# Differential attention scores on all 128 rows of the array, from keys and queries split into high and low parts

## The chip, the cores and the metric

One core of one Trainium2 chip. The metric is the device time of one launch in microseconds (us); lower is better.

## What is computed

One decoder layer on 256 tokens of width 2048, all in float32. Three parts follow each other with residual adds: a mixer with two attention branches, cross-attention into 256 memory tokens, and a gated MLP with a short causal convolution. The change lies in the first branch, differential attention: 8 heads, each with two softmax maps of dimension 64 and values of 128.

```python
z = h @ w_in                       # h: normalised x
qa, ka, va, qb, kb, vb, ga, gb = split_columns(z, IN_WIDTHS)
qa = partial_rope(qa.reshape(b, s, 8, 2, 64), cos, sin)   # first 16 of 64
ka = partial_rope(ka.reshape(b, s, 8, 2, 64), cos, sin)
...
sc = einsum('bhmqd,bhmkd->bhmqk', q, k) * 64 ** -0.5
p = softmax(where(causal, sc, -inf))
a = p[:, :, 0] - lam * p[:, :, 1]
o = einsum('bhqk,bhkv->bhqv', a, v)
```

## The kernel before

**The products.** Every weight product goes through `product` (L208): a unit of 512 output columns, accumulated in two PSUM banks (one per 128 tokens) over 16 blocks of 128 rows. The weights come in pieces of 1 MB on SP's queue. `split_w` (L191) makes two float32r parts of each half piece: ACT casts the high part (L193), DVE subtracts for the low part (L194), and `mm3` (L197) issues three matmuls of 512 columns, high by high, high by low and low by high (L199 to L201). A unit of the mixer has 96 of them; they are called plain matmuls below. The high and low tiles have three buffers each, and PSUM has four banks for products and four (`sm_tile`) for everything small.

**The order.** The program emits a unit, and after every half piece `tick` (L92) advances queued generators (`spawn`, L89) such as one stage of an attention head. The units of the mixer come as qa0, ka0, va0, qa1, ka1, va1, qb0, kb0, vb0, qb1, kb1, vb1 and eight gates. This emitted order is then reordered per engine by a scheduler with a time model of its own (all engines but SP); what stands in a row on an engine is fixed when the program is built, and each engine takes its instructions in that row. A unit reuses the PSUM banks of the unit two before it, so qb0 needs the banks of ka1.

**Queries and keys of branch A.** `proj_T` (L274) scales the two banks on ACT into two SBUF tiles (L280), `rope` (L252) rotates them with four GpSimd operations each, PE transposes four 128x128 blocks per tile (L289), and DVE copies them out (L291). Queries and keys then have features on partitions, head by head, 64 rows per map.

**A head.** `diff_head` (L332) has four stages. Scores: per map two float32 matmuls on 64 rows (L340), of 128 and 256 key columns, then DVE adds the mask (L343) and takes maxima (L346), ACT exponentiates (L352), DVE normalises and subtracts the maps (L354 to L360). Then PE transposes the weights (L322 to L324) and DVE copies them (L326). Then six matmuls with the values (L369 to L371), sums of squares on ACT (L174) and a norm on DVE and ACT (L376 to L388). Last, two transposes (L393) and a split (L398, L399). Two chains of two heads each run after va0 and again after va1.

**Stick-breaking queries and keys.** `proj_F` (L297) does without PE: ACT scales the bank in place, DVE transposes 32x32 blocks (`turn`, L127), and 16 transfers on the GpSimd queue (`regroup`, L131) put the blocks in their places.

Of the kernel before, what the change touches and what calls it, by code (L numbers as in the profile page):

```python
# [9 lines left out]
F32 = mybir.dt.float32  # L10
F32R = mybir.dt.float32r
AF = mybir.ActivationFunctionType
ALU = mybir.AluOpType
# [3 lines left out]
P = 128  # L17
S = 256
NT = S // P
# [4 lines left out]
U = 512  # L24
# [4 lines left out]
ROT = 16  # L29
HALF = ROT // 2  # L30
# [15 lines left out]
def hybrid_layer(ctx: ExitStack, tc: tile.TileContext, x, xT, mem, memT, gmix, par, gfin,  # L46
                 w_in, w_pa, w_pb, w_out, w_xq, w_xkv, w_xo, w_up, w_dn, out):
    nc = tc.nc
# [3 lines left out]
    b4 = ctx.enter_context(tc.tile_pool(name="b4", bufs=34))  # L52
    wk = ctx.enter_context(tc.tile_pool(name="wk", bufs=7))
    st = ctx.enter_context(tc.tile_pool(name="st", bufs=4))
# [14 lines left out]
    ident = cst.tile([P, P], F32, name="ident")  # L69
# [19 lines left out]
    def spawn(gen, delay=0):  # L89
        tasks.append([clock[0] + delay, gen])  # L90
# [16 lines left out]
    def chunk_tile(name, shape):  # L107
        return b4.tile(shape, F32, tag="b4", name=name)

    def sm_tile(name):  # L110
        return ps_sm.tile([P, U], F32, tag="sm", name=name)
# [15 lines left out]
    def turn(blk, src, t):  # L127

        nc.vector.transpose(out=blk[:, :, t * P:(t + 1) * P], in_=src.rearrange("p (f c) -> p f c", c=P))  # L129

    def regroup(dst, blk):  # L131


        q = P // 4
        d, s = (v.rearrange("p f (t c) -> p (f t) c", t=NT) for v in (dst, blk))
        for a in range(4):
            for b in range(4):
                nc.gpsimd.dma_start(out=d[b * q:(b + 1) * q, :, a * q:(a + 1) * q],  # L138
                                  in_=s[a * q:(a + 1) * q, :, b * q:(b + 1) * q])

    def flip_tile(name):
        return chunk_tile(f"{name}_blk", [P, U // P, S])
# [109 lines left out]
    def rope(z, t):  # L252
        v = z.rearrange("p (m d) -> p m d", d=64)
        a = wk.tile([P, 8, ROT], F32, tag="rope", name="rope_a", bufs=2)
        b = wk.tile([P, 8, ROT], F32, tag="rope", name="rope_b", bufs=2)
        c = col("rc", t * ROT, ROT).unsqueeze(1).broadcast_to([P, 8, ROT])
        s = col("rs", t * ROT, ROT).unsqueeze(1).broadcast_to([P, 8, ROT])
        nc.gpsimd.tensor_tensor(out=a, in0=v[:, :, 0:ROT], in1=c, op=ALU.mult)
        nc.gpsimd.tensor_tensor(out=b[:, :, 0:HALF], in0=v[:, :, HALF:ROT], in1=s[:, :, 0:HALF],
                                op=ALU.mult)  # L260
        nc.gpsimd.tensor_tensor(out=b[:, :, HALF:ROT], in0=v[:, :, 0:HALF], in1=s[:, :, HALF:ROT],
                                op=ALU.mult)
        nc.gpsimd.tensor_tensor(out=v[:, :, 0:ROT], in0=a, in1=b, op=ALU.add)

    def proj_T2(ps, r, name):

        dst = [None, None]
        z = chunk_tile(f"{name}_z", [P, NT, U])
        for t in range(NT):
            nc.scalar.activation(out=z[:, t], in_=ps[t], func=AF.Copy, scale=r[:, t:t + 1])  # L270
        spawn(transposed(dst, z, 0, name), 2)
        return dst

    def proj_T(ps, r, name, rotate=False):  # L274

        dst = chunk_tile(name, [P, 4, S])
        zs = []
        for t in range(NT):
            z = wk.tile([P, U], F32, tag="w2", name=f"{name}_z")
            nc.scalar.activation(out=z, in_=ps[t], func=AF.Copy, scale=r[:, t:t + 1])  # L280
            if rotate:
                rope(z, t)
            zs.append(z)

        def rest():
            for t in range(NT):
                pt = sm_tile(f"{name}_tp")
                for h in range(4):
                    nc.tensor.transpose(out=pt[:, h * P:(h + 1) * P],  # L289
                                        in_=zs[t][:, h * P:(h + 1) * P], identity=ident)  # L290
                nc.vector.tensor_copy(out=dst[:, :, t * P:(t + 1) * P],  # L291
                                      in_=pt.rearrange("p (h s) -> p h s", h=4))
            yield 0
        spawn(rest(), 2)
        return dst

    def proj_F(ps, r, name, box, i):  # L297


        blk = flip_tile(name)  # L300
        for t in range(NT):
            nc.scalar.activation(out=ps[t], in_=ps[t], func=AF.Copy, scale=r[:, t:t + 1])
            turn(blk, ps[t], t)

        def rest():
            box[i] = chunk_tile(name, [P, 4, S])
            regroup(box[i], blk)
            yield 0
        spawn(rest(), 1)

# [21 lines left out]
    def diff_head(h):  # L332
        qT, kT, v, hh = qa[h // 4], ka[h // 4], va[h // 4], h % 4

        at = (slice(0, P), slice(P, 3 * P))
        sc = [sm_tile(f"sa{m}") for m in range(2)]
        nm = st.tile([P, 2, NT], F32, tag="nm", name="nm")
        for m in range(2):
            for i in range(NT):
                nc.tensor.matmul(sc[m][:, at[i]], lhsT=qT[m * 64:(m + 1) * 64, hh, i * P:(i + 1) * P],  # L340
                                 rhs=kT[m * 64:(m + 1) * 64, hh, 0:(i + 1) * P], start=True, stop=True)
            dg = sc[m].rearrange("p (i k) -> p i k", i=2)[:, :, 0:P]
            nc.vector.tensor_tensor(out=dg, in0=dg, in1=mask_le.unsqueeze(1).broadcast_to([P, 2, P]),  # L343
                                    op=ALU.add)
            for i in range(NT):
                nc.vector.tensor_reduce(out=nm[:, m, i:i + 1], in_=sc[m][:, at[i]], op=ALU.max,  # L346
                                        axis=AX, negate=True)
        p = [wk.tile([P, 3 * P], F32, tag="w2", name=f"pa{m}") for m in range(2)]
# [42 lines left out]
        pt = sm_tile("oaT")  # L391
# [3 lines left out]
        if oaT[h // 2] is None:  # L395
            oaT[h // 2] = act_tile(f"oaT{h // 2}")
        dst = oaT[h // 2]
        nc.scalar.activation(out=dst[:, 0, j], in_=pt[:, 0:S], func=AF.Copy, scale=gsub)  # L398
        nc.vector.scalar_tensor_tensor(out=dst[:, 1, j], in0=pt[:, 0:S], scalar=gsub,  # L399
                                       in1=dst[:, 0, j].bitcast(F32), op0=ALU.mult,  # L400
# [57 lines left out]
    def unit(u, name, **kw):  # L458
        return product(hT, w_in, u, KD, name, **kw)

    def chain(stage, items):
        for i in items:
            yield from stage(i)
            yield 1
# [7 lines left out]
    pq = unit(0, "qa0", pieces=[1, 1] + [2] * 7, before=first, heap=True)  # L472
# [15 lines left out]
    pk = unit(2, "ka0", before=lambda k0: input_sumsq(x, r0ss, k0 // KB, "r0"))  # L488
    r0 = rstd(r0ss, NT, D, "r0")
    r0a = scaled(r0, 64 ** -0.5, "r0a")  # L490
    r0b = scaled(r0, 128 ** -0.5, "r0b")
    qa, ka, va, qb, kb, vb = ([None, None] for _ in range(6))
    for i in range(2):
        qa[i] = proj_T(unit(i, f"qa{i}") if i else pq, r0a, f"qaT{i}", True)
        ka[i] = proj_T(unit(2 + i, f"ka{i}") if i else pk, r0, f"kaT{i}", True)
        va[i] = proj_n(unit(4 + i, f"va{i}"), r0, f"va{i}")
        spawn(chain(diff_head, (4 * i, 4 * i + 2)))
        spawn(chain(diff_head, (4 * i + 1, 4 * i + 3)), 2)
    for i in range(2):
        proj_F(unit(6 + i, f"qb{i}"), r0b, f"qbT{i}", qb, i)  # L500
        proj_F(unit(8 + i, f"kb{i}"), r0, f"kbT{i}", kb, i)
# [85 lines left out]
    for g in range(2):  # L587
        po = sm_tile("ox").rearrange("p (m s) -> p m s", m=2)
        for m in range(2):
            h = 2 * g + m  # L590
# [171 lines left out]
```

## Time and profile before

| | |
|---|---|
| median of 3 runs | 1493.68 us (1493.48 to 1493.75) |
| profiled execution | 1493.29 us, its span 1491.5 us |
| PE busy | 1475.6 us (99%) |
| DVE, ACT, POOL busy | 929.6, 788.9, 342.7 us |
| HBM traffic | 192 GB/s over the span |

PE's ends are modelled and its matmuls overlap, so its work is read from the spacing of their starts, not from durations. The mixer's first six units, with the heads among them, take the span's first 160 us.

### The profile page before, as it was taken

The page shows a single profiled execution, that of the slowest core. Times are in us where ns is not written, and L with a number is a line of the kernel's source. Part 1 is how long each engine was busy: PE and PEld are TensorE (multiplying, and loading weights), DVE is VectorE, ACT ScalarE, POOL GpSimd, SP SyncE. Part 2 cuts the span into 40 slices and gives each one's busy share as a digit, 9 for nine tenths or more (in the row PEclk, how much of TensorE's full clock was granted, in tenths as well). Part 3 has the DMA queues.
Part 4 walks back from the last instruction along what each step waited for, and adds up shares of the span by engine and source line. Part 5 has one row for each costly group of instructions (what it writes and reads, how often), then busy time and mean ns, then how long its engine had stood idle before and what let it go on. Part 6 is the DMA issues. An engine that isn't in the chain of part 4 may idle for free.

```text
span 1491.5 us, 17974 instructions
## 1 busy us (share of the span) xinstructions
PE 1475.6 (99%) x6648; PEld 1217.4 (82%) x6648; DVE 929.6 (62%) x1219; ACT 788.9 (53%) x1094; POOL 342.7 (23%) x576
## 2 busy tenths in 40 slices
PE   8999999999999999999999999999999999999997
PEld 6878788888888888888888888888888888888886
DVE  5566675655444566775576767767776776645552
ACT  6455555456554444664565555555655555444441
POOL 0202040400000240341004344434434443000010
PEclk9999999999999999999999999999999999999999
DMA  9544455554555566975456666666667666655561
GB/s 350 190 148 170 167 177 193 190 187 163 194 197 192 197 223 227 303 234 204 141 175 215 218 225 224 197 227 217 217 219 225 224 194 228 219 194 198 201 234 73
DMA packets 60391, 304.61 MB, mean 204 GB/s; under 512 B 13200, under 2 KB 13200, under 8 KB 27536
## 3 DMA queue, kind: packets, MB, share of 16 engines
q1 hardware_dynamic: 43488, 286.13, 55.5%
q0 software_dynamic: 16384, 16.81, 4.4%
q8 instruction: 52, 0.85, 0.2%
q10 hardware_dynamic: 432, 0.53, 0.1%
q14 instruction: 35, 0.29, 0.1%
HBM read 284.54 MB, written 2.10 MB: 192 GB/s over the span
## 4 chain that ended last, share of the span: by engine, by line
PE 97%; ACT 1%; issue 1%; DVE 0%; DMA 0%; POOLq 0%; POOL 0%; DVEq 0%; SPq 0%
PE up_mm L201 11%; PE up_mm L200 11%; PE up_mm L199 11%; PE dn_mm L199 5%; PE dn_mm L200 5%; PE dn_mm L201 5%; PE g_mm L200 4%; PE g_mm L201 4%; PE g_mm L199 3%; PE wo_mm L200 2%; PE wo_mm L201 2%; PE wo_mm L199 2%; PE qa_mm L199 1%; PE qa_mm L200 1%; PE va_mm L200 1%; PE qa_mm L201 1%
## 5 line engine op out<-in xcount | busy, mean ns | idle before, releaser
L194 DVE TENSOR_TENSOR up_lo<-up_raw,up_hi 128x1024 fp32r<-128x1024 f32 x176 | 214.5, 1223 | 130.8 <-ACT up_hi L193 130.8
L193 ACT CAST up_hi<-up_raw 128x1024 fp32r<-128x1024 f32 x176 | 184.9, 1051 | 192.3 <-PE up_mm L201 176.0
L201 PE MATMUL up_mm<-up_hi,x2T 128*128 128x512 f32 x704 | 273.9, 389 | 0.0
L200 PE MATMUL up_mm<-up_lo,x2T 128*128 128x512 f32 x704 | 273.9, 389 | 0.0
L138 POOL DMA_DIRECT2D uT<-up_blk x352 | 202.4, 583 | 287.9 <-DVE up_blk L129 188.0
L199 PE MATMUL up_mm<-up_hi,x2T 128*128 128x512 f32 x704 | 246.1, 389 | 0.0
L194 DVE TENSOR_TENSOR dn_lo<-dn_raw,dn_hi 128x1024 fp32r<-128x1024 f32 x88 | 109.8, 1253 | 94.8 <-ACT dn_hi L193 89.7
L200 PEld LDWEIGHTS up_mm<-up_lo,x2T 128*128 128x128 f32 x704 | 132.2, 188 | 27.4
L201 PEld LDWEIGHTS up_mm<-up_hi,x2T 128*128 128x128 f32 x704 | 132.2, 188 | 27.4
L199 PEld LDWEIGHTS up_mm<-up_hi,x2T 128*128 128x128 f32 x704 | 132.2, 188 | 27.3
L193 ACT CAST dn_hi<-dn_raw 128x1024 fp32r<-128x1024 f32 x88 | 91.9, 1054 | 115.1 <-PE dn_mm L201 98.6
L200 PE MATMUL dn_mm<-dn_lo,gT 128*128 128x512 f32 x352 | 136.9, 389 | 0.0
L201 PE MATMUL dn_mm<-dn_hi,gT 128*128 128x512 f32 x352 | 136.9, 389 | 0.0
L194 DVE TENSOR_TENSOR g_lo<-g_raw,g_hi 128x1024 fp32r<-128x1024 f32 x64 | 78.3, 1224 | 83.8 <-ACT g_hi L193 83.8
L199 PE MATMUL dn_mm<-dn_hi,gT 128*128 128x512 f32 x352 | 125.9, 389 | 0.0
L193 ACT CAST g_hi<-g_raw 128x1024 fp32r<-128x1024 f32 x64 | 67.2, 1051 | 70.0 <-PE g_mm L201 64.4
L200 PE MATMUL g_mm<-g_lo,hT 128*128 128x512 f32 x256 | 100.5, 392 | 0.8 <-DVE g_lo L194 0.8
L201 PE MATMUL g_mm<-g_hi,hT 128*128 128x512 f32 x256 | 100.0, 391 | 0.0
L199 PE MATMUL g_mm<-g_hi,hT 128*128 128x512 f32 x256 | 90.2, 389 | 0.0
L201 PEld LDWEIGHTS dn_mm<-dn_hi,gT 128*128 128x128 f32 x352 | 66.1, 188 | 13.8
L199 PEld LDWEIGHTS dn_mm<-dn_hi,gT 128*128 128x128 f32 x352 | 66.1, 188 | 13.8
L200 PEld LDWEIGHTS dn_mm<-dn_lo,gT 128*128 128x128 f32 x352 | 66.1, 188 | 13.6
(310 smaller groups left out, 2783.7 us busy)
## 6 DMA issues: line engine op xcount, KB each, us to landing
up_raw<-in_w_up SPq DMA_DIRECT2D x88, 1024.0 KB, 5.3
dn_raw<-in_w_dn SPq DMA_DIRECT2D x44, 1024.0 KB, 4.9
g_raw<-in_w_in SPq DMA_DIRECT2D x32, 1024.0 KB, 4.9
wo_raw<-in_w_out SPq DMA_DIRECT2D x16, 1024.0 KB, 5.3
uT<-up_blk POOLq DMA_DIRECT2D x352, 32.0 KB, 3.7
ka_raw<-in_w_in SPq DMA_DIRECT2D x8, 1024.0 KB, 6.7
va_raw<-in_w_in SPq DMA_DIRECT2D x8, 1024.0 KB, 4.9
qb_raw<-in_w_in SPq DMA_DIRECT2D x8, 1024.0 KB, 4.9
```

Source lines behind the costliest of these rows:

```text
L138: nc.gpsimd.dma_start(out=d[b * q:(b + 1) * q, :, a * q:(a + 1) * q], in_=s[a * q:(a + 1) * q, :, b * q:(b + 1) * q])
L193: nc.scalar.copy(out=hi, in_=src)
L194: nc.vector.tensor_tensor(out=lo, in0=src, in1=hi.bitcast(F32), op=ALU.subtract)
L199: nc.tensor.matmul(out, lhsT=a[0], rhs=b[0], start=start, stop=False)
L200: nc.tensor.matmul(out, lhsT=a[0], rhs=b[1], start=False, stop=False)
L201: nc.tensor.matmul(out, lhsT=a[1], rhs=b[0], start=False, stop=stop)
```

## The change

Queries and keys of branch A no longer pass through PE transposes. The new `proj_S` scales the PSUM bank in place, rotates it there (`rope` moves from GpSimd to DVE), and turns it in 32x32 blocks on DVE. For keys, ACT and DVE then make a high and a low part of the blocks, and 32 transfers on the GpSimd queue put the parts into one tile per map, with the high part on rows 0 to 63 and the low part on rows 64 to 127. For queries, 32 transfers lay the same blocks into both halves of one tile per map, and ten ticks later ACT and DVE make high and low parts of these tiles. A map's scores are then, for each of the two query blocks, one matmul with the high and one with the low part, both on 128 rows in float32r. The heads are queued four ticks later than before.

```diff
--- before.py
+++ after.py
@@ -255,12 +255,12 @@
         b = wk.tile([P, 8, ROT], F32, tag="rope", name="rope_b", bufs=2)
         c = col("rc", t * ROT, ROT).unsqueeze(1).broadcast_to([P, 8, ROT])
         s = col("rs", t * ROT, ROT).unsqueeze(1).broadcast_to([P, 8, ROT])
-        nc.gpsimd.tensor_tensor(out=a, in0=v[:, :, 0:ROT], in1=c, op=ALU.mult)
-        nc.gpsimd.tensor_tensor(out=b[:, :, 0:HALF], in0=v[:, :, HALF:ROT], in1=s[:, :, 0:HALF],
+        nc.vector.tensor_tensor(out=a, in0=v[:, :, 0:ROT], in1=c, op=ALU.mult)
+        nc.vector.tensor_tensor(out=b[:, :, 0:HALF], in0=v[:, :, HALF:ROT], in1=s[:, :, 0:HALF],
                                 op=ALU.mult)
-        nc.gpsimd.tensor_tensor(out=b[:, :, HALF:ROT], in0=v[:, :, 0:HALF], in1=s[:, :, HALF:ROT],
+        nc.vector.tensor_tensor(out=b[:, :, HALF:ROT], in0=v[:, :, 0:HALF], in1=s[:, :, HALF:ROT],
                                 op=ALU.mult)
-        nc.gpsimd.tensor_tensor(out=v[:, :, 0:ROT], in0=a, in1=b, op=ALU.add)
+        nc.vector.tensor_tensor(out=v[:, :, 0:ROT], in0=a, in1=b, op=ALU.add)
 
     def proj_T2(ps, r, name):
 
@@ -271,29 +271,6 @@
         spawn(transposed(dst, z, 0, name), 2)
         return dst
 
-    def proj_T(ps, r, name, rotate=False):
-
-        dst = chunk_tile(name, [P, 4, S])
-        zs = []
-        for t in range(NT):
-            z = wk.tile([P, U], F32, tag="w2", name=f"{name}_z")
-            nc.scalar.activation(out=z, in_=ps[t], func=AF.Copy, scale=r[:, t:t + 1])
-            if rotate:
-                rope(z, t)
-            zs.append(z)
-
-        def rest():
-            for t in range(NT):
-                pt = sm_tile(f"{name}_tp")
-                for h in range(4):
-                    nc.tensor.transpose(out=pt[:, h * P:(h + 1) * P],
-                                        in_=zs[t][:, h * P:(h + 1) * P], identity=ident)
-                nc.vector.tensor_copy(out=dst[:, :, t * P:(t + 1) * P],
-                                      in_=pt.rearrange("p (h s) -> p h s", h=4))
-            yield 0
-        spawn(rest(), 2)
-        return dst
-
     def proj_F(ps, r, name, box, i):
 
 
@@ -305,6 +282,50 @@
         def rest():
             box[i] = chunk_tile(name, [P, 4, S])
             regroup(box[i], blk)
+            yield 0
+        spawn(rest(), 1)
+
+    def proj_S(ps, r, name, box, i, key):
+
+
+
+        blk = flip_tile(name)
+        for t in range(NT):
+            nc.scalar.activation(out=ps[t], in_=ps[t], func=AF.Copy, scale=r[:, t:t + 1])
+            rope(ps[t], t)
+            turn(blk, ps[t], t)
+
+        def pair(kind, dt):
+            return [b4.tile([P, U // P, S], dt, tag="b4", name=f"{name}_{kind}{m}") for m in range(2)]
+
+        def parts(hi, lo, src):
+            nc.scalar.copy(out=hi, in_=src)
+            nc.vector.tensor_tensor(out=lo, in0=src, in1=hi.bitcast(F32), op=ALU.subtract)
+
+        def place(dst, src):
+            q = P // 4
+            fold = lambda v: v.rearrange("p f (t c) -> p (f t) c", t=NT)
+            for half in range(2):
+                for a in range(4):
+                    for b in range(4):
+                        p0 = 2 * q * half + q * (b % 2)
+                        nc.gpsimd.dma_start(out=fold(dst[b // 2])[p0:p0 + q, :, a * q:(a + 1) * q],
+                                            in_=fold(src[half])[a * q:(a + 1) * q, :, b * q:(b + 1) * q])
+
+        def rest():
+            if key:
+                two = pair("part", F32R)
+                parts(*two, blk)
+                box[i] = pair("st", F32R)
+                place(box[i], two)
+            else:
+                raw = pair("raw", F32)
+                place(raw, [blk, blk])
+                yield 10
+                hi, lo = pair("hi", F32R), pair("lo", F32R)
+                for m in range(2):
+                    parts(hi[m], lo[m], raw[m])
+                box[i] = (hi, lo)
             yield 0
         spawn(rest(), 1)
 
@@ -337,8 +358,9 @@
         nm = st.tile([P, 2, NT], F32, tag="nm", name="nm")
         for m in range(2):
             for i in range(NT):
-                nc.tensor.matmul(sc[m][:, at[i]], lhsT=qT[m * 64:(m + 1) * 64, hh, i * P:(i + 1) * P],
-                                 rhs=kT[m * 64:(m + 1) * 64, hh, 0:(i + 1) * P], start=True, stop=True)
+                for part in range(2):
+                    nc.tensor.matmul(sc[m][:, at[i]], lhsT=qT[part][m][:, hh, i * P:(i + 1) * P],
+                                     rhs=kT[m][:, hh, 0:(i + 1) * P], start=(part == 0), stop=(part == 1))
             dg = sc[m].rearrange("p (i k) -> p i k", i=2)[:, :, 0:P]
             nc.vector.tensor_tensor(out=dg, in0=dg, in1=mask_le.unsqueeze(1).broadcast_to([P, 2, P]),
                                     op=ALU.add)
@@ -491,11 +513,11 @@
     r0b = scaled(r0, 128 ** -0.5, "r0b")
     qa, ka, va, qb, kb, vb = ([None, None] for _ in range(6))
     for i in range(2):
-        qa[i] = proj_T(unit(i, f"qa{i}") if i else pq, r0a, f"qaT{i}", True)
-        ka[i] = proj_T(unit(2 + i, f"ka{i}") if i else pk, r0, f"kaT{i}", True)
+        proj_S(unit(i, f"qa{i}") if i else pq, r0a, f"qaT{i}", qa, i, False)
+        proj_S(unit(2 + i, f"ka{i}") if i else pk, r0, f"kaT{i}", ka, i, True)
         va[i] = proj_n(unit(4 + i, f"va{i}"), r0, f"va{i}")
-        spawn(chain(diff_head, (4 * i, 4 * i + 2)))
-        spawn(chain(diff_head, (4 * i + 1, 4 * i + 3)), 2)
+        spawn(chain(diff_head, (4 * i, 4 * i + 2)), 4)
+        spawn(chain(diff_head, (4 * i + 1, 4 * i + 3)), 6)
     for i in range(2):
         proj_F(unit(6 + i, f"qb{i}"), r0b, f"qbT{i}", qb, i)
         proj_F(unit(8 + i, f"kb{i}"), r0, f"kbT{i}", kb, i)
```

In the built program the order on the engines moves as well. The first place is PE around the heads of the first half. Before, the heads' matmuls stand singly or in small groups between plain matmuls; here the second map of a head and the weight transposes of another (numbers in names are those of buffers), inside unit qa1:

```order
L200 MATMUL qa1_mm1_695<-qa1_lo_741,hT1_140 128x512
L201 MATMUL qa1_mm1_695<-qa1_hi_740,hT1_140 128x512
L340 MATMUL sa1_757<-kaT0_512,qaT0_495 128x128
L340 MATMUL sa1_757<-kaT0_512,qaT0_495 128x256
L199 MATMUL qa1_mm0_694<-qa1_hi_784,hT2_165 128x512
L199 MATMUL qa1_mm1_695<-qa1_hi_784,hT2_165 128x512
L322 MATMUL da_tp_800<-ident_84,pa0_727 128x128
L323 MATMUL da_tp_800<-ident_84,pa0_727 128x128
L324 MATMUL da_tp_800<-ident_84,pa0_727 128x128
L200 MATMUL qa1_mm0_694<-qa1_lo_785,hT2_165 128x512
```

After the change, all of three heads and most of a fourth (54 matmuls by this list, which has a float32 product as one) stand together between the last plain matmul of va1 and the first of qb0; these are the last of them:

```order
L343 MATMUL da_tp_1255<-ident_84,pa0_1187 128x128
L344 MATMUL da_tp_1255<-ident_84,pa0_1187 128x128
L345 MATMUL da_tp_1255<-ident_84,pa0_1187 128x128
L415 MATMUL oaT_1279<-ident_84,o_1236 128x128 x2
L391 MATMUL oa_1285<-va0_739,da_aT_1259 128x128
L392 MATMUL oa_1285<-va0_739,da_aT_1259 128x128
L393 MATMUL oa_1285<-va0_739,da_aT_1259 128x128
L199 MATMUL qb0_mm0_1531<-qb0_hi_1535,hT0_109 128x512
L200 MATMUL qb0_mm0_1531<-qb0_lo_1536,hT0_109 128x512
L201 MATMUL qb0_mm0_1531<-qb0_hi_1535,hT0_109 128x512
```

So three matmuls on values, which need the whole softmax of the last head, now stand ahead of all of qb0. A second group of the same 54, with heads 4 to 7, stands between vb0 and qb1; head 0 (and 4) has its scores 34 plain matmuls ahead of the group.

The second place is DVE. Before, the copies that free PE's transposes stand between low-part subtractions of the weights (L194), two or so per unit; here those of qa0 and ka0 inside va0:

```order
L291 COPY qaT0_495<-qaT0_tp_571 128x4x128
L194 TENSOR_TENSOR va0_lo_608<-va0_raw_589,va0_hi_607 128x1024
L291 COPY kaT0_512<-kaT0_tp_577 128x4x128
L194 TENSOR_TENSOR va0_lo_626<-va0_raw_623,va0_hi_625 128x1024
L291 COPY kaT0_512<-kaT0_tp_583 128x4x128
L194 TENSOR_TENSOR va0_lo_642<-va0_raw_623,va0_hi_641 128x1024
L194 TENSOR_TENSOR va0_lo_660<-va0_raw_657,va0_hi_659 128x1024
L343 TENSOR_TENSOR sa0_714<-sa0_714,mask_le_93 128x2x128
```

After the change, the block transposes of ka1, which free the PSUM banks that qb0 is to use, stand behind the last softmax and the last copy of the group of heads:

```order
L407 TENSOR_TENSOR ro_1229<-ro_1229,st_o_1227 128x2
L410 TENSOR_SCALAR o_1236<-oa_1218,ro_1229 128x128 x2
L347 COPY da_aT_1259<-da_tp_1255 128x384
L129 STREAM_TRANSPOSE kaT1_blk_1322<-ka1_mm0_998 128x4x128
L129 STREAM_TRANSPOSE kaT1_blk_1322<-ka1_mm1_999 128x4x128
L421 SCALAR_TENSOR_TENSOR oaT1_1282<-oaT_1279,gsub_322,oaT1_1282 128x256
L303 TENSOR_TENSOR kaT1_part1_1365<-kaT1_blk_1322,kaT1_part0_1364 128x1024
L398 TENSOR_SCALAR st_o_1294<-ss_o_1289 128x2
L404 TENSOR_TENSOR st_o_1294<-st_o_1294,ro_1296 128x2
L405 TENSOR_TENSOR st_o_1294<-st_o_1294,ro_1296 128x2
```

So the bank of ka1, read here as `ka1_mm0`, comes free only after `da_aT` of the last head. No low-part subtraction of weights stands on DVE between the third one of qb0, early in the group, and the fourth, some rows behind these. In the second group kb0's block transposes stand in the same place.

## Rows read from the trace of the kernel before

**Rows 1.** the page: busy us of the engines; engines of the last chain
```profile
PE 1475.6 (99%) x6648; PEld 1217.4 (82%) x6648; DVE 929.6 (62%) x1219; ACT 788.9 (53%) x1094; POOL 342.7 (23%) x576
...
PE 97%; ACT 1%; issue 1%; DVE 0%; DMA 0%; POOLq 0%; POOL 0%; DVEq 0%; SPq 0%
```

**Rows 2.** waits of PE over the span: us, times, longest us
```profile
PE qa_mm L199 <- ACT qa_hi L193: 5.9, 1, 5.9
```

**Rows 3.** chain, plain matmuls: start us, us, what
```profile
22.77 0.45 PE qa_mm L199 x2
...
25.49 0.45 PE qa_mm L199 x2
```

**Rows 4.** timeline of PE, four transposes: start us, us, what
```profile
50.27 0.60 PE L289 MATMUL qaT_tp<-ident,qaT_z 128*128 128x128 f32 x4
...
50.94 0.40 PE L201 MATMUL ka_mm<-ka_hi,hT 128*128 128x512 f32 x1
```

**Rows 5.** timeline of PE, the scores of one map
```profile
68.05 0.61 PE L199 MATMUL va_mm<-va_hi,hT 128*128 128x512 f32 x2
68.59 0.92 PE L340 MATMUL sa<-kaT,qaT 64*128 64x128 f32 x4
...
69.78 0.39 PE L201 MATMUL va_mm<-va_hi,hT 128*128 128x512 f32 x1
```

**Rows 6.** timeline of PE, two transposes and the scores of two maps
```profile
195.26 0.38 PE L393 MATMUL oaT<-ident,o 128*128 128x128 f32 x2
195.57 0.93 PE L340 MATMUL sa<-kaT,qaT 64*128 64x128 f32 x8
...
196.77 0.39 PE L201 MATMUL kb_mm<-kb_hi,hT 128*128 128x512 f32 x1
```

**Rows 7.** timeline of PE, float32r cross-attention scores
```profile
722.26 0.28 PE L200 MATMUL sx<-kxT,qxT 128*128 128x256 f32 x1
722.38 0.28 PE L201 MATMUL sx<-kxT,qxT 128*128 128x256 f32 x1
```

**Rows 8.** timeline of DVE, one head's masks, maxima and softmax
```profile
196.59 0.75 DVE L343 TENSOR_TENSOR sa<-sa,mask_le 128x256 f32<-128x256 f32 x2
197.25 1.14 DVE L346 TENSOR_REDUCE nm<-sa 128x1 f32<-128x128 f32 x4
...
199.91 0.17 DVE L354 RECIPROCAL sm<-sm 128x4 f32<-128x4 f32 x1
...
201.46 1.23 DVE L194 TENSOR_TENSOR kb_lo<-kb_raw,kb_hi 128x1024 fp32r<-128x1024 f32 x1
```

**Rows 9.** timeline of ACT, a head's first exponential; a head's sums of squares
```profile
198.15 0.36 ACT L352 ACTIVATE pa<-sa,nm 128x128 f32<-128x128 f32 x1
...
205.29 0.28 ACT L174 ACTIVATE junk<-oa 128x128 f32<-128x128 f32 x1 [1.16 <-PE oa L371]
```

**Rows 10.** timeline of DVE, a head's norm and the next copy
```profile
205.95 0.17 DVE L376 TENSOR_SCALAR st_o<-ss_o 128x2 f32<-128x2 f32 x1 [0.56 <-ACT junk L174]
206.62 0.16 DVE L382 TENSOR_TENSOR st_o<-st_o,ro 128x2 f32<-128x2 f32 x1 [0.51 <-ACT ro L381]
...
207.41 0.61 DVE L388 TENSOR_SCALAR o<-oa,ro 128x128 f32<-128x128 f32 x2
207.94 0.55 DVE L326 COPY da_aT<-da_tp 128x384 f32<-128x384 f32 x1
```

**Rows 11.** groups of DVE, 180 to 215 us: block transposes
```profile
L129 DVE STREAM_TRANSPOSE qbT_blk<-qb_mm 128x512 f32<-128x512 f32 x2 | 1.4, 716 | 0.4 <-ACT qb_mm L302 0.4
```

**Rows 12.** groups of POOL: transfers of branch B's queries
```profile
L138 POOL DMA_DIRECT2D qbT<-qbT_blk x32 | 18.6, 589 | 87.9 <-DVE qbT_blk L129 86.7 <-DMA qbT<-qbT_blk 1.1
```

**Rows 13.** windows: PE, PEld, DVE, ACT, POOL busy, granted clock, DMA share, GB/s
```profile
6.00:12.00 6.00, 6.00 (x14) 4.49 (x15) 3.61 (x6) 3.48 (x6) 0.00 (x0) 1.00 1.01 356
12.00:18.00 6.00, 6.00 (x27) 4.89 (x27) 4.84 (x12) 4.75 (x9) 0.00 (x0) 1.00 1.02 397
1483.00:1491.00 8.00, 0.17 (x1) 0.00 (x0) 2.45 (x5) 1.44 (x3) 0.55 (x1) 0.73 0.35 131
```

## The prediction

> **What bounds the kernel now.** I read the page first: PE is busy for 99% of the span and makes up 97% of the chain that ended last [rows 1]. Then PE's waits: the only long one is 5.9 us for the first weights, at the very start [rows 2]. So PE never stands still in the mixer; whatever the heads of branch A wait for is hidden behind plain matmuls. The reader should see in this that two kinds of change count: those in PE's own work, one for one, and those that take the cover away. PE's work is read from starts: 12 plain matmuls lie between two steps of the chain 2.72 us apart [rows 3], so one costs 0.227 us.
>
> **What PE loses.** (a) Transposes. Four of them start at 50.27, and the second plain matmul behind them at 50.94 [rows 4]: 0.67 less one plain matmul is 0.44 for four, 0.11 each. There are 8 such fours: **-3.6 us**. (b) Old scores. After a pair of plain matmuls from 68.05 the one marked L201 would start three steps later, at 68.73; with one map's scores between, it starts at 69.78 [rows 5], so a map alone costs 1.05. Where both maps stand together, 195.26 to 196.77 is 1.51 [rows 6]; less one plain matmul (0.23) and two transposes (0.22) this leaves 1.06 for two maps. So 16 maps cost between 8.5 (all in pairs) and 16.8 (all single). PE's timeline has 14 such groups, the first and the last of them shown; priced group by group, they make **-13.0 us**.
>
> **What PE gains.** A head has 8 float32r matmuls, half with 128, half with 256 columns. Those with 256 follow each other every 0.12 us in cross-attention [rows 7]. No row has 128 columns in float32r. Below, the price is 0.06, half of that; above, 0.22, two float32 halves at the 0.11 of a transpose [rows 4]. I take 0.12, from the row of the same type and the same weight load: about 1.0 per head (0.7 to 1.4).
>
> **Where the heads go.** This decides. The order on PE puts 54 matmuls of four heads behind the last plain matmul of va1 and ahead of the first of qb0, and the same again between vb0 and qb1. An engine takes its instructions in their row, so in these two groups PE stands still while each head's softmax, weights and norm are made on DVE and ACT, and nothing of qb0 can fill in. DVE's row says the same from another side: the bank that qb0 needs is freed by a block transpose behind the last head's copy.
>
> I price a group by following the chain from the end of va1's last matmul. Prices of the legs on DVE: two masks 0.66, or 0.33 each; the maxima of one map 0.53 (four reductions last 1.14, and the end of the last overlaps what follows); from reciprocal to the finished weights 1.55 [rows 8]. The two maps' exponentials take 1.76 with their hand-over (198.15 to 199.91), so 0.85 to 0.95 for one map [rows 8, 9]. Sums of squares take 0.66 up to the norm, Ln and Exp 0.67 to 206.62, then four small operations in a row 0.79, the scaling 0.53, a copy some 0.45 (0.55 long, its end overlapped) [rows 9, 10]. One low-part subtraction of 1.2 is in the group [rows 8].
> - First stretch: scores of the second head and the first transposes on PE 1.5; mask, maxima, subtraction, copy, maxima 2.95; last map's exponentials 0.95; reciprocal to weights, with the norm's first step of the head before, 1.75; four small operations 0.8; scaling and copy 0.95. Together 8.9.
> - Second stretch: value matmuls with their latency 0.65; sums of squares and norm 1.3; masks and maxima of the third head between the norm's steps 1.65; scaling 0.5; exponentials 0.4 not yet covered; reciprocal, output split and weights 1.9. Together 6.4.
> - Third stretch: first half of the fourth head's scores 0.55; masks, maxima, copy 2.1; exponentials 0.95; reciprocal to weights 1.55; wait and four small operations 1.05; scaling and copy 0.95; block transpose of the bank 0.72 [rows 11] and hand-over. Together 7.9.
>
> A group thus takes **23.2 us**, twice: **+46.4**. From below: DVE's own operations in it, added without any wait, are 17.7, and they must run between, since the second head's scores stand behind va1 on PE. From above: some 40 hand-overs at 0.1 more than I gave, and slower matmuls, bring it to 28. I take 23.2 because each leg is a spacing from the trace of the same operations.
>
> What PE does inside is paid already: 11 small matmuls per head at 0.11 are 9.7 for 8 heads, of which all but two pairs of output transposes now lie in the groups: **-9.2**. The scores of heads 0 and 4 stand outside: **+2.0** (1.4 to 2.8).
>
> **The clock.** At the start PE does 14 matmuls in the stretch 6 to 12 us and 27 in the next six [rows 13], half rate, so its clock is at 1.2 GHz there and at 2.4 GHz after; those 13 missing matmuls cost 3.0 us. At the end, with PE silent, the granted clock over the last 8 us averages 0.73, so it has gone to the lower level in them [rows 13]. In a group PE works only some 7 of 23 us (24 scores at 0.12, 42 instructions at 0.11). From below the clock costs nothing, from above 3.0 behind each group and about 1 within it; I take 3.0 each, the row of the start: **+6.0**.
>
> The Trainium skill (TensorE: Matmul & The Clock Gate, Part 1) says that half rate is the default, that activity releases it and an idle stretch brings it back; it gives two levels only. By that page the loss is paid, near my value; if the small matmuls count as enough activity, it is not, and the sum is 6 lower. Rows 13 show a fall only where PE was wholly silent.
>
> **What is hidden.** Rotation on DVE, block transposes and parts replace four copies per half: 16 operations between 0.16 and 0.43 (the small ones in rows 10, a mask in rows 8), four of 0.72, three subtractions of 1.2, together 9 to 13 us on DVE, less the copies, over three units of 21.8 us each. DVE is 62% busy, and weights are split up to three half pieces (8 us) ahead, so I cost this at nothing; without that cover it is at most 5 us per half. ACT's three more casts per half lie in the same slack. GpSimd loses its rotation, which nothing else needed. Its queue gets 128 transfers. At 0.589 each [rows 12] the first 64 take 38 us; the first scores stand 350 plain matmuls, 79 us, behind the start of va0. ka1's 32 take 19 us from the first group's end; their reader comes 254 plain matmuls, 58 us, later. Both are in time. SP's order of weight loads does not change, and its loads only gain time while PE stands.
>
> **The sum.** The profiled execution took 1493.3 us. Less 3.6, 13.0 and 9.2, plus 2.0, 46.4 and 6.0 gives 1521.9; the median of the runs lies 0.4 above that execution: **1522 us**, 1.9% slower.
>
> **The rivals.**
> - *Cheap groups.* Groups near DVE's own 17.7 and no loss of clock: 1493.7 - 23.8 + 35.4 = 1505. Against it: the softmax chain crosses engines at every step; for it: DVE's waits could overlap between the two chains of heads. 12%, from 1505 to 1512.
> - *Dear groups or late keys.* 28 per group and 4 for the clock give 1534. Or the stacked keys land late: GpSimd's issues would have to take over 1.2 us each for the first 64 to miss their 79 us; at 1.4 they would cost about 15 more, 1537. Against: 0.589 under a DVE as busy as here. The Trainium skill (SBUF — State Buffer, SBUF: two separate sides) warns that some DVE operations keep GpSimd from writing the descriptors of its transfers; it would give this rival its way, but the issue times just named already contain it. 10%.
> - *Faster.* PE's work alone: 3.6 and 13.0 off, 8 heads at 1.0 on: 1485. It needs groups that cost less than (25.8 - 2.0) / 2 = 11.9 us each; that is the point that decides. The change of PE's own work is real, and it would win if the heads stood between plain matmuls as before. Against: DVE alone needs 17.7. 2%.
>
> **How the numbers follow.** The forecast, 1512 to 1534, has 75%; with cheap groups 12, dear ones 10, faster 2, and 1 for about no change. A measurement of this kernel can tell some 0.2% from no change. The range of 8 in 10 reaches a little into the cheap and the dear case: 1509 to 1535. Faster 0.02, same 0.01, slower 0.97.
>
> **What would show it.** In the changed profile: PE's waits list some 20 us for DVE and ACT around matmuls of `da_tp`, `oa` and `oaT`, twice, near 140 and 225 us; the granted clock dips behind each; a run of scores without the transposes' fours; POOL's issues at about 0.6. The forecast is wrong if PE's row shows plain matmuls inside those stretches, if the two gaps are below 12 us, or if PE waits for a transfer ahead of `sa`.

## The result and the profile after

The changed kernel takes **1526.62 us** (median of 4 runs, 1526.1 to 1527.38) against 1493.72 (1493.48 to 1493.79): a ratio of 1.0223, 95% interval 1.0211 to 1.0235, so 2.2% slower. Predicted were 1522 and 1509 to 1535. The profiled execution took 1527.38 us with a span of 1525.5, 34.0 more than before.

The page, busy us of the engines and the engines of the last chain, to be read beside [rows 1]:

```profile
PE 1485.4 (97%) x6616; PEld 1227.4 (80%) x6616; DVE 943.2 (62%) x1257; ACT 796.4 (52%) x1100; POOL 398.2 (26%) x672
...
PE 94%; DVE 2%; ACT 2%; issue 1%; DMA 1%; SPq 0%; POOLq 0%; POOL 0%; DVEq 0%; ACTq 0%
```

PE has fewer matmuls than before and yet lost two points of its share, and DVE's and ACT's shares of the chain have grown from 0 and 1% to 2% each. PE's waits (us in total, times, longest us) name the place; in [rows 2] none of them stood:

```profile
PE oa L391 <- DVE da_aT L347: 6.4, 4, 2.5
PE da_tp L343 <- DVE pa L382: 6.3, 4, 1.8
PE oaT L415 <- DVE o L410: 6.1, 6, 1.9
...
PE da_tp L343 <- DVE st_o L398: 2.2, 2, 1.1
PE vb_mm L199 <- DVE qbT_blk L129: 1.4, 1, 1.4
PE g_mm L199 <- ACT gate L336: 1.0, 1, 1.0
```

The first four, 21 us, lie in the two groups of heads. PE's timeline shows the bounds of the first group, its stretches and what follows it (start us, us, what, idle before and its releaser):

```profile
140.74 0.27 PE L343 MATMUL da_tp<-ident,pa 128*128 128x128 f32 x1
...
149.56 0.77 PE L391 MATMUL oa<-va,da_aT 128*128 128x128 f32 x2
...
156.96 0.47 PE L343 MATMUL da_tp<-ident,pa 128*128 128x128 f32 x1 [1.68 <-DVE pa L382]
...
164.75 0.66 PE L415 MATMUL oaT<-ident,o 128*128 128x128 f32 x2 [0.66 <-DVE o L410]
...
166.74 0.77 PE L199 MATMUL qb_mm<-qb_hi,hT 128*128 128x512 f32 x1
...
169.81 0.39 PE L200 MATMUL qb_mm<-qb_lo,hT 128*128 128x512 f32 x1
...
234.68 0.27 PE L343 MATMUL da_tp<-ident,pa 128*128 128x128 f32 x1
...
260.84 0.77 PE L199 MATMUL qb_mm<-qb_hi,hT 128*128 128x512 f32 x1
...
265.51 0.39 PE L201 MATMUL qb_mm<-qb_hi,hT 128*128 128x512 f32 x1
```

So a group lasts 26.0 us (140.74 to 166.74) and 26.2 us (234.68 to 260.84). Behind the first, seven plain matmuls take 3.07 us instead of 1.59, behind the second eleven take 4.67 instead of 2.50. The windows (PE, PEld, DVE, ACT, POOL busy, granted clock, DMA share, GB/s) tell why:

```profile
140.00:146.00 6.00, 3.06 (x21) 2.45 (x20) 4.48 (x10) 2.88 (x10) 0.00 (x0) 0.99 0.52 175
146.00:152.00 6.00, 4.09 (x17) 3.31 (x17) 3.81 (x16) 2.02 (x11) 0.00 (x0) 0.50 0.01 3
152.00:158.00 6.00, 2.37 (x12) 1.92 (x11) 4.73 (x20) 2.70 (x11) 0.00 (x0) 0.78 0.01 3
158.00:164.00 6.00, 4.20 (x17) 3.00 (x15) 4.43 (x17) 2.87 (x14) 0.00 (x0) 0.50 0.00 0
```

The clock falls to its lower level (1.2 GHz) inside the group, not only behind it. (In the second group it is at 0.50 in all three windows from 240 to 258 us.) The chain of waits shows what that costs there: these are the first and the last of PE's own pieces on the path from the fall to the end of the group (start us, us, what).

```profile
148.84 0.66 PE oaT L415 x2
149.56 0.77 PE oa L391 x2
...
157.44 0.87 PE sa L362 x4
...
166.23 0.43 PE oa L392 x2
166.66 0.43 PE oa L393 x2
```

The chain has ten of them, 5.9 us in all. A pair of 128-column products that took 0.22 at two of the transposes' 0.11 [rows 4] takes 0.43 here, so about half of it, some 3.0 us, is the clock's; an estimate from these rows, which no run measures by itself. Without it the group would last some 23.0.

**Where the 34.0 us of the span come from**: -25.8 for the work that left its old places (the prediction's price, not measured by itself), +1.8 for heads 0 and 4, +52.2 for the two groups, +3.7 for the half rate behind them, and +2.4 for the two new waits of `vb_mm` and `g_mm`. That makes 34.3.

**Why the heads stand so late.** The view of the tile of stacked keys (ns min, median, max; first and last start us) and its landing times, both of 20 to 150 us:

```profile
L312 POOL DMA_DIRECT2D kaT_st<-kaT_part x32: 575/582/615, 72.6 to 95.1; - x32
...
DMA to landing us min/median/max: 2.2/3.8/6.2
```

The keys have landed by 102 us at the latest, and the low parts of the queries end at 94.5. The first scores stand at 132.10: some 30 us, 130 plain matmuls, after their data. PE's row was fixed at build time, and the build had placed them there; PE itself did plain matmuls up to them.

### The profile page after: what moved, and what is told of

Same layout as the page of the kernel before. It is cut to its first block, busy times and chain, and to the rows that moved or that the text cites. A ratio compares the mean times of both kernels' runs of the same rounds, so it can differ in the third digit from the quotient of the medians.

```text
span 1525.5 us, 18090 instructions
## 1 busy us (share of the span) xinstructions
PE 1485.4 (97%) x6616; PEld 1227.4 (80%) x6616; DVE 943.2 (62%) x1257; ACT 796.4 (52%) x1100; POOL 398.2 (26%) x672
## 4 chain that ended last, share of the span: by engine, by line
PE 94%; DVE 2%; ACT 2%; issue 1%; DMA 1%; SPq 0%; POOLq 0%; POOL 0%; DVEq 0%; ACTq 0%
PE up_mm L199 10%; PE up_mm L201 10%; PE up_mm L200 10%; PE dn_mm L200 5%; PE dn_mm L201 5%; PE dn_mm L199 5%; PE g_mm L200 3%; PE g_mm L199 3%; PE g_mm L201 3%; PE wo_mm L200 2%; PE wo_mm L201 2%; PE wo_mm L199 2%; PE qb_mm L199 1%; PE qb_mm L201 1%; PE qb_mm L200 1%
## 5 line engine op out<-in xcount | busy, mean ns | idle before, releaser
L194 DVE TENSOR_TENSOR up_lo<-up_raw,up_hi 128x1024 fp32r<-128x1024 f32 x176 | 214.4, 1223 | 130.8 <-ACT up_hi L193 130.8
L194 DVE TENSOR_TENSOR dn_lo<-dn_raw,dn_hi 128x1024 fp32r<-128x1024 f32 x88 | 109.7, 1252 | 94.9 <-ACT dn_hi L193 89.7
L194 DVE TENSOR_TENSOR g_lo<-g_raw,g_hi 128x1024 fp32r<-128x1024 f32 x64 | 78.2, 1223 | 83.8 <-ACT g_hi L193 83.8
L200 PEld LDWEIGHTS dn_mm<-dn_lo,gT 128*128 128x128 f32 x352 | 66.0, 188 | 13.7
```

What stands on the lines that cost most here:

```text
L194: nc.vector.tensor_tensor(out=lo, in0=src, in1=hi.bitcast(F32), op=ALU.subtract)
L200: nc.tensor.matmul(out, lhsT=a[0], rhs=b[1], start=False, stop=False)
```

## The experiments

Theory A: the loss is PE standing in the two groups, so it is a matter of the order; the change of PE's own work is a gain. Theory B: the work that was added to DVE, ACT and the queues costs this wherever the heads stand. Theory C: a part is the clock. All runs stand beside runs of the kernel before on the same chip, whose medians were 1493.1 to 1493.3.

| run | us | ratio to before, 95% |
|---|---|---|
| 1 heads later | 1493.98 | 1.0005 (0.9996 to 1.0014) |
| 2 heads some later | 1504.54 | 1.0074 (1.006 to 1.0088) |
| 3 kernel before, heads later | 1494.36 | 1.0008 (0.9999 to 1.0016) |
| 4 blocks alone, heads later | 1493.70 | 1.0004 (0.9995 to 1.0012) |
| 5 fillers | 1538.86 | 1.0302 (1.0288 to 1.0316) |
| 6 PE by hand | 1526.98 | 1.0221 (1.0207 to 1.0235) |
| 7 kernel before, PE by hand | 1523.51 | 1.0202 (1.0188 to 1.0216) |
| 8 blocks, PE by hand | 1521.26 | 1.0186 (1.0172 to 1.02) |
| 9 queries on ACT's queue | 1525.38 | 1.0214 (1.0199 to 1.023) |
| 10 the same, later | 1525.02 | 1.0214 (1.0199 to 1.0229) |
| 11 blocks as queued | 1494.58 | 1.0011 (1.0001 to 1.002) |
| 12 stages apart | **1486.67** | **0.9956 (0.9942 to 0.9969)** |

**Run 1.** The changed kernel with two other numbers: how many ticks later the two chains of heads are queued.

```diff
-        spawn(chain(diff_head, (4 * i, 4 * i + 2)), 4)
-        spawn(chain(diff_head, (4 * i + 1, 4 * i + 3)), 6)
+        spawn(chain(diff_head, (4 * i, 4 * i + 2)), 20)
+        spawn(chain(diff_head, (4 * i + 1, 4 * i + 3)), 22)
```

> The changed kernel with the two chains of heads queued 20 and 22 ticks behind va0 (va1) instead of 4 and 6; nothing else. In the order that this gives, every head's matmuls on PE stand between plain matmuls of va1 to vb1, and no group of 54 is left. Theory A (the loss is PE standing in the two groups; the work of PE itself has become cheaper): the heads and transposes of before cost PE 26.4 us by their spacing of starts, the same without transposes and with new scores at 0.93 a head cost 8 x 0.93 + 9.7 = 17.1, so the time falls to 1493.7 - 26.4 + 17.1 = 1484, up to 1488 if a few short waits stay. Theory B (the loss is in what the change adds: rotation, block transposes and parts on DVE, casts on ACT, 128 transfers, float32r scores): that work is all still there, so at least half of the 33 us stays, 1510 or more.

Measured 1493.98. All added work is still there, and 32.6 of the 33 us are gone, so theory B in its plain form falls. But A's 1484 is missed by 10 us. Its waits on PE:

```profile
PE kb_mm L199 <- ACT va L336: 1.8, 1, 1.8
PE g_mm L199 <- DVE kbT_blk L129: 1.8, 1, 1.8
PE sb_tp L344 <- ACT ab L456: 1.7, 1, 1.7
PE g_mm L199 <- ACT gate L336: 1.4, 1, 1.4
PE sb L436 <- DVE st_o L404: 1.3, 1, 1.3
```

The last heads now stand among those of branch B (`sb`), and banks come free late: 8.0 us of waits that [rows 2] don't have. Whether these are what is missing, runs 6 to 12 were to tell.

**Run 2.** The same with 8 and 10.

> The changed kernel with the heads queued 8 and 10 ticks later instead of 4 and 6. In its order a part of the first group is left (30 matmuls: the second and third heads' scores, two heads' weight transposes and values, ahead of the first matmul of qb0), and the second group is gone. Theory A: the part lasts about 10.3 us on the trace of the changed kernel (140.74 to 151.1), of which 3.5 would be paid anyway, so 1484 + 6.8, with up to 1.5 for the clock behind it: 1490 to 1493. Theory B: as for the previous kernel, 1510 or more.

Measured 1504.54: between the two, as A has it, but 11 us over its range. The rest of the first group shows in the second and third row, which the expectation had; the first and the fourth, 6.0 us of banks that come free late, it had not. The part of the group also lasted 12.0 us (140.76 to 152.72) instead of 10.3, and the granted clock falls once more behind those waits (0.74 over 184 to 190 us).

```profile
PE kb_mm L199 <- ACT va L336: 4.2, 1, 4.2
PE oa L391 <- DVE da_aT L347: 2.5, 1, 2.5
PE da_tp L343 <- DVE pa L382: 1.8, 1, 1.8
PE kb_mm L199 <- ACT vb L336: 1.8, 1, 1.8
```

**Run 3**, the control: the kernel before with the heads queued with 20 and 22 instead of 0 and 2.

> The kernel before with its heads queued 20 and 22 ticks later instead of 0 and 2: a control. Theory A: there was no standing PE to be gained, so nothing changes but how the old scores stand: more of them have both maps together, which cost 1.06 for two maps where single maps cost 1.05 each; 1489 to 1494. Theory B': queueing later is itself worth 8 us or more in any kernel (1486 or less), so that the first run of this study would say nothing of the change.

Measured 1494.36, no gain: queueing later is worth nothing where PE does not stand. So run 1's 32.6 us belong to the groups of the changed kernel.

**Run 4.** `proj_S` without parts: `rest` regroups the blocks into one tile, as in `proj_F`, and `diff_head` keeps the old scores; heads with 20 and 22.

> Half of the change, with the heads queued 20 and 22 ticks later: rotation in PSUM, block transposes and 16 transfers per tensor on the GpSimd queue, but queries and keys stay whole and the scores are the old float32 ones on 64 rows. Theory A: against the kernel before with late heads it saves the 8 fours of transposes, 3.6 us, and the rest of the gain is the scores': 1487 to 1491. Theory B: rotation and block transposes on DVE and the transfers cost more than the transposes on PE gave, 1494 or more.

Measured 1493.70, 0.7 under run 3 where 3.6 were expected, and between the two ranges. PE has no wait of half a us or more here that it doesn't have in run 3, so the blocks did not hold it up. On PE's row the old scores stand at 16 places here and at 10 in run 3; by the starts, these places with what stands beside the scores cost about 18 and 15.4 us. So a price per map carries over to another order only roughly.

**Run 5.** Six 128-column matmuls behind a head's scores and behind its weight transposes, four of 256 columns behind its value matmuls, into unused columns; nothing reads them.

```diff
+    def idle(out, n):
+        for _ in range(n):
+            nc.tensor.matmul(out, lhsT=hT[0][:, 0, 0, 0:P], rhs=hT[0][:, 0, 0, 0:out.shape[-1]],
+                             start=True, stop=True)
...
+            if m:
+                idle(sc[m][:, 3 * P:4 * P], 6)
```

> The changed kernel with matmuls added in every head whose results nothing reads (into unused columns of the banks that the head has anyway): 6 of 128 columns behind a head's scores, 6 behind its weight transposes, 4 of 256 columns behind its value matmuls. The order is otherwise that of the changed kernel, so the two groups are still there and hold 42 more matmuls of 128 and 16 of 256 columns each. Theory C (a part of the 26.6 us of a group is PE's half rate inside it, since 54 small matmuls at the granted clock of 0.5 are spaced 0.21 where they are 0.11 before): the added work of 4.4 us a group by the full rate's spacings falls into waits, PE has more to do, the clock falls later or not at all, and a group shrinks to 21 to 25 us; time 1517 to 1525. Rival: the clock stays at half all the same, then the fillers take 8.9 us a group, of which some 3 to 5 don't fit into the waits; time 1530 to 1540.

Measured 1538.86: the rival's case. The first group grew from 26.0 to 31.9 us (PE's timeline), and the clock fell all the same, only later (windows as above):

```profile
141.74 0.27 PE L348 MATMUL da_tp<-ident,pa 128*128 128x128 f32 x1
...
173.61 0.61 PE L199 MATMUL qb_mm<-qb_hi,hT 128*128 128x512 f32 x1
```

```profile
141.00:147.00 6.00, 4.79 (x37) 4.26 (x36) 4.19 (x9) 2.68 (x8) 0.00 (x0) 1.00 0.54 175
147.00:153.00 6.00, 4.25 (x21) 3.56 (x22) 3.70 (x15) 1.60 (x9) 0.00 (x0) 0.77 0.01 3
...
159.00:165.00 6.00, 4.95 (x23) 4.79 (x23) 3.38 (x11) 1.63 (x8) 0.00 (x0) 0.50 0.00 0
```

So the run doesn't price the clock; that price rests on the chain of the changed kernel above, and theory C stays an estimate.

**Runs 6 to 8.** PE's row as the program emits it, heads with 16 and 18: the changed kernel, the kernel before, and the half of run 4.

```diff
-    with tile.TileContext(nc, schedule_with_timeline_sim=True) as tc, tc.manual_schedule(engines={mybir.EngineType.SP}):
+    with tile.TileContext(nc, schedule_with_timeline_sim=True) as tc, tc.manual_schedule(engines={mybir.EngineType.SP, mybir.EngineType.PE}):
```

> The changed kernel with PE's order written as the program emits it (PE taken out of the scheduler's hands, as SP is), and heads queued 16 and 18 ticks later: one stage of a head stands between every 12 or 24 plain matmuls, from the end of ka1 to the middle of qb0, and again from the end of kb0 to the middle of qb1. Theory A: the first run of this study did not reach 1484 because its heads were pushed among those of branch B and waited 8 us for banks and scores; here these waits are gone: 1484 to 1488. Theory B: the added work on DVE and ACT takes what PE gains wherever the heads stand, so that the 8 us return at other places: 1491 to 1496.

> The kernel before with PE's order as the program emits it, and the heads queued as in the kernel by hand above: the control to it. Here the scores of both maps always stand together. By the rows of before, two maps cost 1.06 together and 1.05 alone, so PE's small work is 3.6 for transposes, 8.5 for scores and 9.2 for the rest, 21.3 against 26.4: 1487 to 1490, and the change of the kernel is worth some 4 us in this order, not 9. Rival: placing is worth nothing to the old scores, 1493 to 1495, and the change is worth 8 or more.

> Half of the change with PE's order as the program emits it and the heads queued as in the two kernels above: rotation in PSUM, block transposes and 16 transfers per tensor, with the old float32 scores on 64 rows. If scores of both maps standing together cost 1.06 a head in float32 against 0.93 in parts, this kernel saves the transposes' 3.6 us and lies 1 us behind the changed one by hand: 1485 to 1487. Rival: the scores in parts are what the change gains by, then it lies 4 us or more behind it.

Measured 1526.98, 1523.51 and 1521.26: all three expectations wrong by 30 us or more. PE's waits in run 6, then in run 7:

```profile
PE sb_tp L344 <- ACT ab L456: 12.0, 3, 4.9
PE oa L391 <- DVE da_aT L347: 9.0, 2, 8.8
PE da_tp L343 <- DVE pa L382: 6.6, 4, 4.5
```

```profile
PE sb_tp L323 <- ACT ab L434: 12.0, 3, 4.9
PE oa L369 <- DVE da_aT L326: 6.9, 2, 6.7
```

The program's own distances (12 plain matmuls, 2.7 us, between a head's transposes and its values; all six `sb_tp` 36 behind `sb`) are too short for the legs on DVE and ACT. The kernel before, with not one operation changed, loses 30 us by its order alone, nearly as much as the changed kernel in that order (34). That is theory A from the other side. In one and the same order the blocks save 2.3 us, near the transposes' 3.6; what the parts are worth these runs don't tell, as run 6 waits more than run 7.

**Runs 9 and 10.** Run 1's idea with the heads early: the queries' transfers go out on ACT's queue, and the heads are queued with 10 and 12 (run 10: 14 and 16).

```diff
-        def place(dst, src):
+        def place(dst, src, eng):
...
-                        nc.gpsimd.dma_start(out=fold(dst[b // 2])[p0:p0 + q, :, a * q:(a + 1) * q],
+                        eng.dma_start(out=fold(dst[b // 2])[p0:p0 + q, :, a * q:(a + 1) * q],
...
-                place(raw, [blk, blk])
+                place(raw, [blk, blk], nc.scalar)
```

> The changed kernel with the queries' 32 transfers per half issued on ACT's queue (the keys' stay on the GpSimd queue) and the heads queued 10 and 12 ticks later. In the order this gives, the heads start in ka1 instead of va1, no two stages of a head stand next to each other without plain matmuls between, and all heads are done before those of branch B. Theory A (the time is set by what PE finds to do between a head's stages): no groups, no collision with branch B; PE's small work for branch A is 17 to 18 us against the 26.4 of before: 1484 to 1488, faster than the kernel before. Theory B (the added work on DVE, ACT and the queues costs about what PE gains, wherever the heads stand): 1492 or more, the more so as ACT now issues 64 transfers too.

> The kernel above with the heads queued 14 and 16 ticks later: again single stages between plain matmuls, but the last head of the second half now ends among branch B's first. Theory A: as above, with a few waits like those of the first run of this study (7 us there, where two heads stood among branch B's): 1486 to 1491. Theory B: 1492 or more.

Measured 1525.38 and 1525.02. No wait of a head is left on PE; two others are as long as the whole loss. PE's waits in run 9, and ACT's timeline:

```profile
PE ka_mm L199 <- ACT ka_hi L193: 17.6, 1, 17.6
PE va_mm L199 <- ACT va_hi L193: 16.6, 1, 16.6
```

```profile
53.16 21.78 ACTq L312 DMA_DIRECT2D qaT_raw<-qaT_blk  x31
74.99 1.04 ACT L302 CAST kaT_part<-kaT_blk 128x1024 fp32r<-128x1024 f32 x1 [21.03 <-DMA qaT_raw<-qaT_blk]
75.94 2.93 ACT L193 CAST va_hi<-va_raw 128x1024 fp32r<-128x1024 f32 x3
```

ACT issues 31 transfers in 21.8 us, 0.70 each, and the weight casts stand behind them: what the GpSimd queue does for nothing costs 34.2 us here. The Trainium skill (SBUF — State Buffer, SBUF: two separate sides) advises ACT's or SP's queue where DVE keeps GpSimd from writing descriptors. In the changed kernel POOL issues the same 64 transfers at 0.586 each, as in [rows 12], so there was nothing of that kind to win. Behind these waits plain matmuls run at half rate: the first 12 take 5.45 us (77.03 to 82.48) instead of 2.72, and behind the second wait some 2.8 more are lost. Without the waits and this, run 9 would be near 1486, where A has it; that is an estimate, and run 12 is the test.

**Run 11.** Run 4's kernel in the change's own queueing, 4 and 6.

> Half of the change in the change's own queueing (4 and 6 ticks): rotation in PSUM, block transposes and 16 transfers per tensor, with the old float32 scores. In its order the heads start in qa1, and all but a few stages have plain matmuls between them; only at the end of va1 four stages stand together. Theory A: it is the doubled transfers and the parts that moved the heads to the end of va1 (vb0) in the changed kernel; without them no group, so nearly all of the 33 us is gone: 1491 to 1498. Theory B: rotation and block transposes on DVE carry a good part of the loss: 1505 or more.

Measured 1494.58, inside A's range. With half the transfers, no parts and none of the ten ticks ahead of the queries' parts, the build places the heads early, and there is no group. Which of the three moved them is not shown; nor is it that the build takes the 64 transfers for slower than they are.

**Run 12.** The changed kernel with the stages of heads and pairs further apart; all transfers on the GpSimd queue.

```diff
-        yield 2
+        yield 4
         aT = attn_T(aw, "da")
-        yield 1
+        yield 2
...
-        yield 2
+        yield 4
         pt = sm_tile("oaT")
...
-        yield 3
+        yield 5
         aT = [attn_T(aw[m], "sb") for m in range(2)]
-        yield 1
+        yield 3
...
+        spawn(chain(diff_head, (4 * i, 4 * i + 2)), (22, 14)[i])
+        spawn(chain(diff_head, (4 * i + 1, 4 * i + 3)), (23, 15)[i])
```

> The changed kernel, all transfers on the GpSimd queue as in the change, with the stages of a head (and of branch B's pairs) queued further apart: 4, 2 and 4 ticks between a head's stages instead of 2, 1 and 2, 5 and 3 instead of 3 and 1 in branch B, the two chains of heads 22 and 23 ticks behind va0, 14 and 15 behind va1. In the order this gives, no stage of a head stands close behind the stage that it needs: 14 plain matmuls at the least, and mostly 20 to 50. Theory A (the whole loss, and the 7 us of waits left in the first run of this study, is what PE waits between a head's stages and for banks; the work added to DVE, ACT and the queues costs nothing by itself): with the first run's waits gone, 1494 - 7 = 1487, or by PE's work alone 1484; I expect 1482 to 1488, faster than the kernel before. Theory B (added work takes what PE gains, wherever the heads stand): 1492 or more, with the waits at other places.

Measured **1486.67**, faster than both kernels. PE's waits above half a us, to be read beside [rows 2]:

```profile
PE qa_mm L199 <- ACT qa_hi L193: 6.6, 2, 5.7
PE kb_mm L199 <- ACT va L336: 2.2, 1, 2.2
PE wo_mm L200 <- DVE wo_lo L194: 0.8, 1, 0.8
```

One new wait of 2.2 us is left, and 1484 of PE's work alone (an estimate) plus 2.2 is 1486. DVE's, ACT's and POOL's added work is all in this kernel, and nothing of it shows beyond that wait. Theory A holds, B falls. Not tried: the kernel before with these distances, of which branch B's are a part. It has no waits to lose [rows 2], but its scores might stand more cheaply, so how much of the 6.7 us is the change's own work stays open.

## Why the prediction was right, and where its terms were off

The mechanism was as forecast: two groups on PE's row, into which no plain matmul fills in. The forecast was 4.6 us too low, 5.5 beside the profiled execution. By the sum over the span the terms were 5.7 too low: 5.8 in the groups and 2.4 in the two new waits, less 2.3 that I had put too much behind the groups and 0.2 in the scores. That the last two cover a part of the others is luck.

- **PE's loss and gain** (-25.8, +2.0). The sum over the span closes to 0.3 us with -25.8, which supports it. The scores of head 0 run from 132.10 to 133.02 between plain matmuls, 0.92 a head for my 1.0, on PE's timeline: a first product of 128 columns takes 0.06, its second 0.11. My bounds of 0.06 and 0.22 held.

```profile
132.10 0.22 PE L362 MATMUL sa<-kaT_st,qaT_hi 128*128 128x128 f32 x1
132.16 0.28 PE L362 MATMUL sa<-kaT_st,qaT_lo 128*128 128x128 f32 x1
132.27 0.33 PE L362 MATMUL sa<-kaT_st,qaT_hi 128*128 128x256 f32 x1
...
133.02 0.40 PE L200 MATMUL va_mm<-va_lo,hT 128*128 128x512 f32 x1
```

- **The groups** (46.4 by my legs, 52.2 measured). They stand where the order showed them, and nothing of qb0 or qb1 fills in. My stretches of 8.9, 6.4 and 7.9 measured 8.8 (to 149.56), 7.4 (to 156.96) and 9.8. The legs on DVE and ACT were right within some tenths. What I had too short are PE's pieces at the lower clock: the value matmuls that open the second stretch (149.56 to 151.2, 1.65 for my 0.65) and the scores of the third with one transpose (156.96 to 158.3, 1.35 for my 0.55). The third also ended elsewhere: not on the block transpose of ka1's bank, which DVE had finished by 166.54, but on PE's own last transposes and values, 164.75 to 166.74.

```profile
165.24 1.30 DVE L129 STREAM_TRANSPOSE kaT_blk<-ka_mm 128x512 f32<-128x512 f32 x2
```

- **The clock** (6.0). This is the term that was mis-sized and misplaced: 3.7 behind the groups where I put 6.0, but some 3 within each where I put 1 as a bound and then left it out. I took 3.0 from the start of the span, where PE does plain matmuls (half rate by their spacing alone: [rows 13] has a granted clock of 1.00 beside 14 matmuls in 6 us); in a group PE's small matmuls are links of the chain, so half rate lengthens the chain itself. The Trainium skill (TensorE: Matmul & The Clock Gate, Part 1) says that half rate is the default and that activity releases it. The trace agrees: with plain matmuls in a row again, the granted clock is 1.00 over 170 to 176 us. The trace adds that full rate is lost in a stretch where PE works on small matmuls between waits: 0.50 from 158 to 164.
- **What is hidden.** Right for DVE, ACT and the transfers, as far as run 12 shows. POOL's issues took what I gave them, and no scores waited for a transfer. Two waits in branch B and the gates, 2.4 us, I had not seen: the order there moved too. Of my signs one was off: I expected some 20 us of waits on PE in each group, and the list has 21 for both. PE counts as busy for 13.7 of the 24 us from 140 to 164.
- **The rivals.** "Faster, 1485", with the heads between plain matmuls, is what run 12 shows at 1486.67. My price for it was near, and so was the reason why the change as made doesn't get there.

## What to carry to other kernels

Where one engine is full, read the built order before the operations: a change that gained 7 us in one order lost 33 in another, because a dependent chain stood alone on the engine's row. Ask for each stage what stands between it and the stage that it needs; mostly 20 to 50 plain matmuls (5 to 11 us), 14 at the least, were enough here, 12 were not. When data comes later by a new path, move the consumer in the emitted program as well, and keep transfers off the queue of an engine that others wait for.

## What was not expected of the hardware

- The granted clock falls inside a group, though PE has matmuls there: near 146 us in the first, where PE had been busy for 1.1 of the last 4 us. It comes back for a few us and falls again (0.50, 0.78, 0.50 in three windows of 6 us); in the second group it doesn't come back. In run 5, with more matmuls in the same places, it was 0.50 over 159 to 165 us as well.
- An issue on ACT's queue took 0.70 us of ACT's time on the mean (31 in 21.78 us), more than the 0.586 of one on GpSimd's, and from the end of the cast at 53.95 to 74.94 us nothing else of ACT ran.
